# Sums over keys through DRAM into all lanes before the reciprocal, and the mix two slots later

## The chip, the cores and the metric

The kernel runs on one core of one Trainium2 chip. The metric is the device time of one execution in microseconds (us). A core has five engines that the profile names PE (TensorE; PEld are its weight loads), DVE (VectorE), ACT (ScalarE), POOL (GpSimd) and SP (SyncE, which issues every DMA of this kernel). Data lies in SBUF, in PSUM (where PE writes its products) and in DRAM.

## The reference

One layer of a bidirectional encoder, for two sequences: `prompt` with 1024 tokens and `sample` with 2048, of width 1024. The tokens are normalised and projected once; the projection is cut into a pooling mixer, a self-attention with 8 heads of 64 on 2 key heads, a cross-attention of 4 heads into 256 memory tokens, and a gate for each. The gated results are concatenated, projected, normalised and added to the input. What matters here is the softmax of both attentions, and what follows it:

```
s = jnp.einsum('bqkgd,bskd->bkgqs', qblk, k, preferred_element_type=jnp.float32) * scale
p = jax.nn.softmax(s, axis=-1)
return jnp.einsum('bkgqs,bskd->bqkgd', p.astype(v.dtype), v)
...
attn_out = block_self_attention(q, k, v) * jax.nn.silu(g_attn)
...
mix = jnp.concatenate([pool_out, attn_out, x_out], axis=-1)
y = jnp.einsum('bte,ed->btd', mix, w_out)
return x + rms_norm(y, norm_post)
```

## The kernel before

**Stages.** A first stage (about 700 us) normalises and projects all tokens and leaves queries, keys, values and gates in DRAM. The second stage, some 1180 us, does attention, the output projection and the last norm. The change lies in the second.

**Groups and slots.** A `Pair` is 256 tokens; there are 8 pairs of the sample and then 4 of the prompt. Each pair has three `Group`s: kind 0 and kind 1 (self-attention of one key head each) and kind 2 (cross-attention). A group goes over its keys in chunks of 128: 16 chunks for a self-attention group of the sample, 8 for one of the prompt, 2 for kind 2. One chunk of one group is a slot; 344 slots, numbered from 0, follow each other. In the first pair the order is kind 2, 0, 1, in the others 0, 2, 1. A pair of the sample has 34 slots, one of the prompt 18. The groups are numbered from 0 as well; group 9 is kind 0 of the fourth pair (slots 102 to 117), group 10 its kind 2 (118, 119) and group 11 its kind 1 (120 to 135).

**A slot.** For one chunk, `weights` (L212) makes scores S on PE in two halves (L220, or L224 for kind 2) and ACT takes their exponential P (L227) out of PSUM, one half each. The halves have two PSUM buffers. One slot later `sums` (L229) adds P to the running sum z, on DVE alone for the prompt and half on POOL, half on DVE for the sample (L239, L240). In most slots `largest` (L177) also prepares a later group: PE makes scores N (L191, or L183 for kind 2) and DVE reduces them to their largest value (L194). N has two PSUM buffers. Every fourth slot, `values` (L242) multiplies four chunks of P with V on PE (L252); below this is called a value slot.

**The end of a group.** Counted from its first slot n with c chunks: in slot n + c + 1 `totals` (L256) sums z over the partitions on PE (L260) into `zt`, which takes one of the two N buffers. In slot n + c + 2 `take` (L264) multiplies the accumulated values with the gate on DVE (L266), and `inverse` (L269) has DVE take the reciprocal of 128 x 256 elements of `zt` (L272; the 32 lanes of each quarter hold the same sums, so 4 lanes tell all), stores 4 lanes to DRAM (L274) and reads them back, broadcast to 64 lanes each, as `gz` (L278). In slot n + c + 5, or later where the pair before still uses the `mix` tile, `mix_out` (L280) has POOL multiply (L288) and then, one to two slots later, ACT rounds the product (L289) and POOL subtracts for the low part (L290; the instructions themselves carry L416).

**The output projection.** `open_fill` (L423) puts the pieces of a pair's projection on a list, 9 slots after the pair's last slot (L436). Two tiles of 128 tokens each have two halves h of 8 pieces, and a piece is three matmuls (L357 to L359). After each half stands a pause: a slot that takes none. Each slot takes n pieces, so many that the list is done by slot `until`: the pieces left, divided by the slots left less the pauses left, rounded up (L892; `until` is set in L426). For the sample, `until` is the first slot of the next pair + 26, for the prompt + 16 (HOLD, L397). When a half is done in slot s, ACT copies it into the tile y at the end of slot s (`half_out`, L365), squares it in slot s + 1 (L370), and when both halves are there DVE prepares the norm in slot s + 2 (L375) and POOL finishes its root (L63); in slot s + 3 `out` has DVE scale y (L383), POOL add it to `xr`, the input read again (L386), and SP store that. The tiles y and xr have one buffer each (L340, L342): the first half of the next tile cannot be copied before POOL's addition for the tile before is done.

**What sets the order.** The second stage is emitted under a written-out order for PE, ACT, DVE and POOL, which run it as it stands. Within a slot it is: S of half 0 and its exponential; the sums of the chunk before; `largest`; what is due at the slot; S of half 1 and its exponential; the pieces of the projection; what is due at slot + 0.5 (END). SP is not in that list: the order of the DMAs is the planner's, by its own simulated times. The two lines that place the calls on the list, as they stand before:

```
            wait = max(first[g] + g.chunks + 5, free)
            at(wait + END, g.mix_out, wait + END, pair)
        at(max(ends) + 9, open_fill, pair, max(ends) + 9)
...
        at(n + c + 2 + END, g.inverse)
```

Here `free` is the slot from which the mix tile can be used: the pair's first slot + 26 (sample) or + 16 (prompt), and 12 for the first pair.

Of the kernel before, what the change touches and what calls it, by code (L numbers as in the profile page):

```python
# [7 lines left out]
F32 = mybir.dt.float32  # L8
# [15 lines left out]
def encoder(ctx, tc, I, O):  # L24


    nc = tc.nc


    dram = ctx.enter_context(tc.tile_pool(name="scratch", bufs=1, space=DRAM))  # L30
# [102 lines left out]
    class Group:  # L133
# [134 lines left out]

        def inverse(self):  # L269

            r = dbl.tile([128, 256], F32, name="rz", tag="rz", bufs=1)
            nc.vector.reciprocal(out=r, in_=self.zt[:, 0:256])  # L272
            rows = dram.tile([4, 256], F32, name="rows", tag="rows", bufs=4)
            nc.sync.dma_start(out=rows, in_=r[0:128:32])  # L274
            self.gz = dbl.tile([128, 512], F32, name="gz", tag="gz")
            for j in range(2):
                src = rows[2 * j:2 * j + 2].rearrange("l q -> (l q)").unsqueeze(0)
                nc.sync.dma_start(out=self.gz[64 * j:64 * j + 64], in_=src.broadcast_to([64, 512]))  # L278
# [13 lines left out]
    class Pair:  # L292
# [15 lines left out]
        def pool(self, slot):  # L308
            self.mix = [own.tile([128, NC, 2, 128], F32R, name="mix", tag=f"mix{hl}") for hl in range(2)]
            store_mix(slot, self, 0, self.u.rearrange("p c q -> p (c q)"),  # L310
                      self.g.rearrange("p c t q -> p (c t q)"))
# [96 lines left out]
    END = 0.5  # L408

    def at(slot, f, *args):  # L410

        later.setdefault(slot, []).append((f, args))
# [5 lines left out]
    first = {}  # L418
# [9 lines left out]
    for pair in pairs:  # L428
        ends = [first[g] + g.chunks - 1 for g in pair.groups]
        at(min(ends), pair.load_pool)  # L430
        free = 12 if pair is pairs[0] else first[pair.groups[0]] + HOLD[pair.s]
        at(max(min(ends) + 4, free), pair.pool, max(min(ends) + 4, free))
        for g in pair.groups:
            wait = max(first[g] + g.chunks + 5, free)
            at(wait + END, g.mix_out, wait + END, pair)
        at(max(ends) + 9, open_fill, pair, max(ends) + 9)  # L436
    for g in groups:
        n, c = first[g], g.chunks
        at(n + END, g.load_late)
        for k in range(0, c, RUN):  # L440
            ks = list(range(k, min(k + RUN, c)))
            at(n + ks[-1] + 1 + END, g.values, ks)
        at(n + c + 1 + END, g.totals)
        at(n + c + 2, g.take)
        at(n + c + 2 + END, g.inverse)
    for c in range(NC):
        at(4 + 3 * c, load_w_out, c)
        at(7 + 3 * c, split_w_out, c)
# [4 lines left out]
    looks, n = {}, len(slots)  # L453
# [406 lines left out]
    dbl = pool("p2two", 2)  # L860
# [14 lines left out]
    with tc.manual_schedule(engines=order):  # L875
        slot = 0
        while slot < len(slots) or later or fill:
            g, k = slots[slot] if slot < len(slots) else (None, 0)
# [13 lines left out]
            n = -(-(len(fill) - pauses) // max(1, until[0] - slot - pauses)) if fill else 0  # L892
            for _ in range(n):
                x = fill.pop(0)
                if x is None:
                    break
                out, h, c, start, final = x
# [57 lines left out]
```

## Time and profile before

| what | value |
|---|---|
| median of 3 runs | 1884.9 us (1884.27 to 1885.07) |
| the profiled execution | 1885.09 us, of which its span is 1883.0 us |
| mean granted PE clock in it | 0.991 |
| busy, share of the span | PE 96%, DVE 60%, POOL 45%, ACT 37% |

Times in the trace count from the span's start. A row of a timeline gives the start, the duration, the engine, the line, the operation, what it writes and reads, the shape, how many instructions were merged into the row, and, in brackets, how long the engine sat idle before it and who ended that. A row of a table of groups gives the count behind an x, then the summed busy time, the mean duration of one in ns, and the idle time before them. A row of the waits gives who waited for whom, the sum, the number of times and the longest. A row of the windows gives the stretch and its length, then the busy time and the number of instructions for PE, PEld, DVE, ACT and POOL, then the granted PE clock, the share of the DMA engines and GB/s. Matmuls overlap in the trace: rows of 0.39 us start 0.23 us apart.

### The profile page before, as it was taken

How to read it: one execution, taken by the hardware profiler on the slowest of the kernel's cores; microseconds unless marked ns; L12 is line 12 of the kernel's file. 1: busy time of each engine (PE TensorE's matmuls, PEld its weight loads, DVE VectorE, ACT ScalarE, POOL GpSimd, SP SyncE). 2: the span in 40 equal slices, each digit the busy share in tenths (PEclk: the TensorE clock that was granted, in tenths of full speed). 3: DMA queues.
4: the chain of work that ended last, by engine and by line, in shares of the span. 5: the costliest groups of instructions: out<-in, count | busy, mean ns of one | idle time of the engine just before them, and what ended most of it. 6: DMA issues, size and time to landing. Idle time of an engine off the chain costs nothing. (4 is left out here: it accounts for less than half of the span.)

```text
span 1883.0 us, 23531 instructions
## 1 busy us (share of the span) xinstructions
PE 1816.8 (96%) x8520; PEld 1282.0 (68%) x8520; DVE 1131.4 (60%) x1304; ACT 697.3 (37%) x1266; POOL 856.7 (45%) x756
## 2 busy tenths in 40 slices
PE   7999999999999998999999999999999999999996
PEld 6888888988988874465564656556565656565564
DVE  7755146431545167867768676767868576756743
ACT  5523233222422115434434343444434343433331
POOL 3665017520546008845638374664837461413313
PEclk9999999999999999999999999999999999999998
DMA  7634454254433926212122220212222242223211
GB/s 243 201 113 121 109 160 132 76 162 110 116 113 102 216 70 167 68 30 79 46 79 62 70 64 25 79 45 79 62 74 62 67 132 64 91 84 100 86 40 62
DMA packets 148485, 181.83 MB, mean 97 GB/s; under 512 B 21505, under 2 KB 118417, under 8 KB 148369
## 3 DMA queue, kind: packets, MB, share of 16 engines
q1 hardware_dynamic: 148368, 180.33, 33.6%
q8 instruction: 67, 1.10, 0.3%
q14 instruction: 50, 0.40, 0.1%
HBM read 126.50 MB, written 53.62 MB: 96 GB/s over the span
## 5 line engine op out<-in xcount | busy, mean ns | idle before, releaser
L227 ACT ACTIVATE P<-S 128x512 f32<-128x512 f32 x688 | 399.3, 598 | 558.3 <-PE S L220 436.2
L194 DVE TENSOR_REDUCE nb<-N 128x1 f32<-128x1024 f32 x256 | 311.6, 1218 | 240.3 <-PE N L191 239.5
L239 POOL TENSOR_TENSOR z<-z,P 128x512 f32<-128x512 f32 x224 | 316.9, 1415 | 223.7 <-ACT P L227 218.8
L252 PE MATMUL acc<-P,V 128*64 128x512 f32 (+1 forms) x1472 | 320.8, 578 | 0.5
L220 PE MATMUL S<-qa,KA 128*128 128x512 f32 x640 | 275.0, 430 | 9.2 <-ACT P L227 9.2
L240 DVE TENSOR_TENSOR z<-z,P 128x512 f32<-128x512 f32 (+1 forms) x272 | 273.6, 1006 | 12.7 <-ACT P L227 12.3
L63 POOL TENSOR_TENSOR rs<-rs,mhalf 128x1 f32<-128x1 f32 (+2 forms) x100 | 100.4, 1007 | 386.2 <-DVE rs L61 386.1
L220 PE MATMUL S<-qb,KB 65*128 65x512 f32 x640 | 254.5, 398 | 0.0
L548 PE MATMUL pz<-hT_hi,w_hi 128*128 128x512 f32 x592 | 233.2, 394 | 1.4 <-ACT vmst L806 0.8
L549 PE MATMUL pz<-hT_lo,w_hi 128*128 128x512 f32 x592 | 232.3, 392 | 0.0
L550 PE MATMUL pz<-hT_hi,w_lo 128*128 128x512 f32 x592 | 232.1, 392 | 0.2 <-DVE w_lo L69 0.2
L191 PE MATMUL N<-KA,qa 128*128 128x512 f32 x640 | 208.1, 406 | 18.4 <-DVE rz L272 11.7
L252 PEld LDWEIGHTS acc<-P,V 128*64 128x64 f32 x1472 | 98.6, 138 | 180.3 <-issue 171.2
L220 PEld LDWEIGHTS S<-qa,KA 128*128 128x128 f32 x640 | 120.4, 188 | 143.6 <-issue 72.5
L194 DVE TENSOR_REDUCE top<-N 128x1 f32<-128x1024 f32 (+1 forms) x88 | 107.0, 1218 | 96.7 <-PE N L191 76.9
L191 PEld LDWEIGHTS N<-KA,qa 128*128 128x128 f32 x640 | 116.9, 191 | 61.7 <-DVE nb L194 22.1
L548 PE MATMUL pz<-w_hi,hT_hi 128*128 128x384 f32 (+1 forms) x416 | 140.3, 338 | 1.4 <-ACT hT_hi L68 1.4
L549 PE MATMUL pz<-w_lo,hT_hi 128*128 128x384 f32 (+1 forms) x416 | 139.9, 336 | 1.0 <-DVE w_lo L69 0.9
L550 PE MATMUL pz<-w_hi,hT_lo 128*128 128x384 f32 (+1 forms) x416 | 140.1, 338 | 0.0
L357 PE MATMUL py<-wo_hi,mix 128*128 128x512 f32 x352 | 137.7, 391 | 0.0
L358 PE MATMUL py<-wo_lo,mix 128*128 128x512 f32 x352 | 137.6, 391 | 0.0
L359 PE MATMUL py<-wo_hi,mix 128*128 128x512 f32 x352 | 137.4, 390 | 0.0
(116 smaller groups left out, 2487.9 us busy)
## 6 DMA issues: line engine op xcount, KB each, us to landing
wraw<-w_in SPq DMA_DIRECT2D x15, 1536.0 KB
dg<-gst SPq DMA_DIRECT2D x48, 256.0 KB
qa<-dq SPq DMA_DIRECT2D x48, 256.0 KB
gz<-rows SPq DMA_DIRECT2D x72, 128.0 KB
x<-x_sample SPq DMA_DIRECT2D x16, 512.0 KB
xr<-x_sample SPq DMA_DIRECT2D x16, 512.0 KB
y_sample<-xr SPq DMA_DIRECT2D x16, 512.0 KB
dq<-qst SPq DMA_DIRECT2D x96, 64.0 KB
```

Of the source, the lines that this page charges most:

```text
L191: nc.tensor.matmul(S[:, 512 * b:512 * b + 512], lhsT=q, rhs=KA[self.kind][:, k:k + 512], start=True, stop=True)
L194: nc.vector.tensor_reduce(out=out, in_=S, axis=AX.X, op=ALU.max, negate=True)
L220: nc.tensor.matmul(S, lhsT=K[self.kind][rows_, keys], rhs=q, start=n == 0, stop=n == 1)
L227: nc.scalar.activation(out=self.P[k][:, j], in_=S, func=AF.Exp)
L239: nc.gpsimd.tensor_tensor(out=z[:, :cut], in0=a[:, :cut], in1=P[:, :cut], op=ALU.add)
L240: nc.vector.tensor_tensor(out=z[:, cut:], in0=a[:, cut:], in1=P[:, cut:], op=ALU.add)
L252: nc.tensor.matmul(self.acc[64 * j:64 * j + 64, x], lhsT=v, rhs=P[:, j, x], start=(k, i) == (0, 0), stop=k == self.chunks - 1, skip_group_ ...
L357: nc.tensor.matmul(ps, lhsT=mh, rhs=wo_hi[:, c, cols], start=first, stop=False)
L358: nc.tensor.matmul(ps, lhsT=mh, rhs=wo_lo[:, c, cols], start=False, stop=False)
L548: nc.tensor.matmul(ps, lhsT=sh, rhs=mh, start=c == 0, stop=False)
L549: nc.tensor.matmul(ps, lhsT=sh, rhs=ml, start=False, stop=False)
L550: nc.tensor.matmul(ps, lhsT=sl, rhs=mh, start=False, stop=c == n - 1)
```

## The change

`inverse` no longer has DVE take the reciprocal in place. ACT copies `zt` to SBUF, 4 lanes go to DRAM, and come back as a tile `rz` of 128 lanes with 8 columns each. A new call `spread`, two slots later, has DVE take the reciprocal of these 128 x 8 elements, stores them to DRAM and reads them back broadcast, as before. `mix_out` and `open_fill` are put two slots later to make room.

```
         def inverse(self):
 
-            r = dbl.tile([128, 256], F32, name="rz", tag="rz", bufs=1)
-            nc.vector.reciprocal(out=r, in_=self.zt[:, 0:256])
+            t = dbl.tile([128, 256], F32, name="zs", tag="zs", bufs=1)
+            nc.scalar.copy(out=t, in_=self.zt[:, 0:256])
+            sums = dram.tile([4, 256], F32, name="zrows", tag="zrows", bufs=4)
+            nc.sync.dma_start(out=sums, in_=t[0:128:32])
+            self.rz = dbl.tile([128, 8], F32, name="rz", tag="rz")
+            nc.sync.dma_start(out=self.rz, in_=sums.rearrange("l (p x) -> (l p) x", x=8))
+
+        def spread(self):
+            r = self.rz
+            nc.vector.reciprocal(out=r, in_=r)
             rows = dram.tile([4, 256], F32, name="rows", tag="rows", bufs=4)
-            nc.sync.dma_start(out=rows, in_=r[0:128:32])
+            nc.sync.dma_start(out=rows.rearrange("l (p x) -> (l p) x", x=8), in_=r)
             self.gz = dbl.tile([128, 512], F32, name="gz", tag="gz")
...
-            wait = max(first[g] + g.chunks + 5, free)
+            wait = max(first[g] + g.chunks + 7, free)
             at(wait + END, g.mix_out, wait + END, pair)
-        at(max(ends) + 9, open_fill, pair, max(ends) + 9)
+        at(max(ends) + 11, open_fill, pair, max(ends) + 11)
...
         at(n + c + 2 + END, g.inverse)
+        at(n + c + 4 + END, g.spread)
```

## The prediction

> **What bounds the kernel now.** I read the page first, then PE's waits by stage, then the timeline around the waits for the reciprocal, then the granted clock there.
>
> ```profile
> span 1883.0 us, 23531 instructions
> PE 1816.8 (96%) x8520; PEld 1282.0 (68%) x8520; DVE 1131.4 (60%) x1304; ACT 697.3 (37%) x1266; POOL 856.7 (45%) x756
> ```
>
> PE is busy nearly all the time, so a change is worth what it adds to or takes from PE's gaps, and what a gap does to PE's pace. The waits of PE, first for 700 to 1630 us (mostly the sample), then for 1630 us to the end (the prompt):
>
> ```profile
> PE N L191 <- DVE rz L272: 5.8, 10, 0.6
> ...
> PE N L191 <- DVE rz L272: 5.9, 3, 2.0
> ```
>
> These 11.7 us are all that PE waits for the reciprocal: `zt` holds one of the two N buffers until DVE is done. Ten waits are short; three, at the last group of a prompt pair, are long. The next rows show one of those, and a value slot's matmuls undisturbed; then the windows of the half clock after each of the three:
>
> ```profile
> 1706.05 0.39 PE L220 MATMUL S<-qb,KB 65*128 65x512 f32 x1
> 1708.40 1.22 PE L191 MATMUL N<-KA,qa 128*128 128x512 f32 x2 [1.96 <-DVE rz L272]
> 1710.41 5.41 PE L252 MATMUL acc<-P,V 128*64 128x512 f32 x16
> ...
> 1621.79 3.65 PE L252 MATMUL acc<-P,V 128*64 128x512 f32 x16
> ```
> ```profile
> 1635.50:1638.90 3.40, 3.40 (x10) 0.99 (x10) 3.37 (x5) 0.60 (x1) 0.00 (x0) 0.50 0.32 97
> 1707.20:1714.00 6.80, 5.60 (x14) 2.29 (x16) 6.77 (x7) 0.60 (x1) 0.00 (x0) 0.50 0.47 147
> 1782.30:1789.00 6.70, 5.79 (x14) 2.40 (x16) 6.65 (x7) 0.60 (x1) 0.13 (x1) 0.50 0.45 143
> ```
>
> PE works in those windows for 3.40, 5.60 and 5.79 us at clock 0.50, so half of it is lost: 1.7, 2.8 and 2.9 us, together 7.4, on top of the 5.9 us of waiting. A gap of 2 us costs another 2.5 us on average (7.4 / 3).
>
> **The reciprocal leaves DVE's long slot.**
>
> ```profile
> L272 DVE RECIPROCAL rz<-N 128x256 f32<-128x256 f32 x36 | 62.9, 1748 | 4.4 <-PE N L260 3.6 <-DMA rows<-rz 0.8
> L609 ACT COPY z<-pz 128x256 f32<-128x256 f32 x24 | 9.3, 386 | 0.0
> L240 DVE TENSOR_TENSOR z<-z,P 128x1024 f32<-128x1024 f32 x48 | 66.6, 1388 | 9.6 <-ACT P L227 9.3
> L194 DVE TENSOR_REDUCE top<-N 128x1 f32<-128x1024 f32 x64 | 77.7, 1217 | 76.9 <-PE N L191 76.9
> ```
> ```profile
> 1017.41 1.19 ACT L227 ACTIVATE P<-S 128x512 f32<-128x512 f32 x2 [0.28 <-PE S L220]
> 1018.69 1.75 DVE L272 RECIPROCAL rz<-N 128x256 f32<-128x256 f32 x1
> 1020.49 0.73 PE L191 MATMUL N<-KA,qa 128*128 128x512 f32 x2 [0.61 <-DVE rz L272]
> ```
>
> DVE gives back 1.75 us in each of 36 groups. Its 8 columns are 8/256 of 1748 ns, 0.05 us; with an estimate for the start I take 0.15. ACT gains a copy, 0.39 us by L609. It stands behind the first of the two exponentials of 1017.41 and ends near 1018.4, two microseconds before the reciprocal's end at 1020.44, and PE's N at 1020.49 goes on without the 0.61 us. The second exponential ends 0.39 us later, at 1019.0; were PE to wait for it, that is 0.4 us in a group at most. So the ten short waits go: **minus 5.8 us**. The three long ones and their half clock are worth 13.3 us (5.9 + 7.4), but DVE there has 2.6 us of work in each slot (the sum of L240, 1.39 us, and the reduction of L194, 1.22) against 1.4 us on PE (six matmuls 0.23 us apart), and catches up now also because PE stands still. I hand back 0.6 us for each, **minus 11.5 us**, with bounds of 8 and 13.3.
>
> **The new trip, and DVE's wait at `spread`.** The trip as it is, from store to use:
>
> ```profile
> 1020.46 0.56 SPq L274 DMA_DIRECT2D rows<-rz  x1
> 1022.12 1.10 SPq L278 DMA_DIRECT2D gz<-rows  x2
> 1025.66 1.28 POOL L288 TENSOR_TENSOR o<-o,gz 128x512 f32<-128x512 f32 x1 [3.54 <-DMA gz<-rows]
> ```
>
> The store takes 1.66 us until the next DMA may start, the broadcast 3.0 us from its second issue (1022.63). The new first half takes 1.66 us and then, for 4 KB in pieces of 32 bytes, which no row shows, between these two: 3.4 to 4.7 us from 1018.4, to some 1023. DVE comes to `spread` behind the reduction of slot n + c + 4, near 1022.4, so it waits up to 0.7 us (more if SP first issues a gate load). Behind DVE stand a sum and a reduction, but this is the value slot, in which PE is busy for 3.65 us; I count nothing, and up to 0.7 us for each prompt pair in the bound above. The second half ends 6 us later, before POOL's multiply two slots later, so POOL's wait of 3.54 us goes, worth nothing on PE.
>
> Once the cover is gone: group 0, while the weights load.
>
> ```profile
> 715.30 1.22 DVE L194 TENSOR_REDUCE nb<-N 128x1 f32<-128x1024 f32 x1
> 716.62 0.54 SPq L274 DMA_DIRECT2D rows<-rz  x1
> 724.53 1.10 SPq L278 DMA_DIRECT2D gz<-rows  x2
> 721.86 0.63 PE L191 MATMUL N<-KA,qa 128*128 128x512 f32 x2
> 708.00:722.00 14.00, 12.81 (x57) 6.80 (x50) 11.41 (x12) 6.87 (x12) 6.56 (x5) 1.00 1.03 267
> ```
>
> The DMA engines are full until 722, and a 4 KB store took 7.9 us (716.62 to 724.53). DVE's `spread` stands behind the reduction of 715.30. If the sums are back at 725, a sum and a reduction later (2 us) PE gets its N buffer at 727 instead of 721.86: 5 us, and 2 for the clock. If the copy's earlier store slips ahead of the loads, nothing. **Plus 5 us**, between 0 and 8.
>
> **The mix and the projection two slots later.** This moves POOL's multiply, ACT's rounding and POOL's low part, but the mix of a pair's first two groups is mostly held by `free` anyway. It also moves where the projection's pieces lie. Take the third pair: its list opened in slot 110 and must be done by 128. Before, slots 111 on took 3, 3, 2, 3, 3, 2 pieces; after a pause the next half began in 118. The first tile was done in 116, its `out` came in 119, and the second tile's first half was done in 121. Now it opens in 112: 32 pieces in 128 - 113 - 4 = 11 slots gives 3, and from 113 on 3, 3, 2, 3, 3, 2, 3, 3, 2. The first tile is done in 118, its `out` comes in slot **121**, and the second tile's first half is done in slot **121** as well. ACT's copy of that half must wait until POOL has added the first tile (one y buffer). Slots 119, 121 and 122 as they were:
>
> ```profile
> 1066.06 0.51 PE L224 MATMUL S<-qa,KA 128*128 128x256 f32 x2
> 1067.31 1.22 DVE L194 TENSOR_REDUCE nb<-N 128x1 f32<-128x1024 f32 x1 [4.52 <-PE N L191]
> 1068.45 1.27 DVE L383 SCALAR_TENSOR_TENSOR y<-y,rs,npost 128x1024 f32<-128x1024 f32 x1
> 1069.81 2.79 POOL L386 TENSOR_TENSOR xr<-xr,y 128x1024 f32<-128x1024 f32 x1 [6.39 <-DVE y L383]
> 1074.62 0.50 PE L220 MATMUL S<-qa,KA 128*128 128x512 f32 x1
> 1077.78 0.59 ACT L365 COPY y<-py 128x512 f32<-128x512 f32 x1 [0.86 <-PE py L359]
> 1078.16 0.50 PE L220 MATMUL S<-qa,KA 128*128 128x512 f32 x1
> 1079.66 0.43 PE L220 MATMUL S<-qa,KA 128*128 128x512 f32 x1
> 1080.68 0.73 PE L191 MATMUL N<-KA,qa 128*128 128x512 f32 x2 [0.36 <-DVE nb L194]
> 1083.10 0.40 PE L220 MATMUL S<-qa,KA 128*128 128x512 f32 x1
> ```
>
> POOL's addition ended 6.54 us after the start of `out`'s slot (1066.06 to 1072.60). Put `out` into slot 121: ACT's copy starts 6.54 us after that slot's start instead of 3.16 (1077.78 - 1074.62), and ends at 7.13. Behind it on ACT stands the first exponential of slot 122, 0.60 us, at 7.73, and for its buffer waits PE's first S of slot 123, which is due 5.04 us after the start of slot 121 (1079.66 - 1074.62). Slot 122 is the pause, so PE has nothing else: a gap of 2.7 us. Slot 123 (1079.66 to 1083.10, 3.44 us) has 0.65 us more than its 12 matmuls need (2.79), a wait behind DVE's reciprocal and reduction that disappears in the gap; net 2.05 us. To this comes the clock, 2.5 us by the three windows, as this gap is longer than theirs: 4.5 us. The same count of slots holds for the second to seventh pair. In the first, `out` comes in 52 and the copy at the end of 53, a slot of cover. **Plus 27 us** (6 x 4.5), 18 to 33 for gaps of 2.1 to 3.3 us and 1.7 to 2.9 for the clock.
>
> The Trainium skill weighs against the clock's part: "TensorE: Matmul & The Clock Gate", section "Why this matters for your kernels", advises no PE-idle gaps over about 3 us, one idle window bringing the clock back to half. By that, a gap of 2.7 us keeps the full clock. This trace disagrees: three gaps of 2.0 us out of three were followed by clock 0.50.
>
> For the four pairs with 8 pieces to a slot (the last of the sample, three of the prompt) the same copy already waits:
>
> ```profile
> 1603.54 0.58 ACT L365 COPY y<-py 128x512 f32<-128x512 f32 x1 [5.62 <-POOL xr L386]
> 1604.68 0.50 PE L220 MATMUL S<-qa,KA 128*128 128x512 f32 x1 [0.54 <-ACT P L227]
> ```
>
> Eight pieces, 5.5 us of matmuls (24 x 0.23), hide it but for half a microsecond. There the pieces now fill four slots in a row; the copy comes one slot later, behind as many pieces: zero, within 4 us in all. In the last pair all pieces come at the end:
>
> ```profile
> 1860.47 1.29 POOL L416 TENSOR_TENSOR mix<-o,mix 128x512 fp32r<-128x512 f32 x1 [0.73 <-ACT mix L416]
> ...
> 1872.18 0.39 PE L359 MATMUL N<-wo_hi,mix 128*128 128x512 f32 x1
> ```
>
> The 24 matmuls that need the last mix are the last, 5.4 us up to 1872.4, so from 1867 on; it is there at 1861.8. DVE's `take` sets the start of both trips, and the new one has 5 us to spare: zero.
>
> **Sum.** -5.8 - 11.5 + 5 + 27 = +14.7. The profiled execution, 1885.1 us, is 0.2 over the median of 1884.9, so the prediction is 1899.6.
>
> **Rivals.**
> *The copy is not held.* If POOL's addition ended 3.4 us sooner, the six gaps vanish: 1885 - 17.3 + 5 = 1873, faster. For it: in 40 of its 44 copies ACT waits for PE's pieces, in four for POOL. Against: those four are just the ones whose `out` comes in the copy's own slot. It decides once the addition ends less than 4 us after the slot's start. 0.13.
> *The gaps come without the half clock.* Then 6 x 2.05 = 12.3 stands against 12.3 of net gain: 1885, no change. This is what the cited page's rule makes of it; three windows speak against. 0.08.
> *DVE's wait at `spread` becomes the bound.* If the trip takes 8 us, the 11 groups at a pair's end past group 0's pair hold DVE 4 us in the value slot, of which 2 are hidden: 2 us and the clock each, +50: 1949. The 1.66 us of the store speaks against. 0.06.
> *The early copy doesn't free the buffer sooner* (held by something later): no gain, 1885 + 5 + 27 = 1917. 0.05.
> My forecast has 0.68.
>
> **Chances and range.** A difference under 0.2% (3.8 us) can't be told from none here. Slower 0.68 + 0.06 + 0.05 = 0.79, same 0.08, faster 0.13. My sum's own bounds: 1885 + 18 + 0 - 19 = 1884 to 1885 + 33 + 8 - 14 = 1912; with 1917 of the last rival, 1883 to 1917 leaves out 0.13 + 0.06.
>
> **What would show it.** Right: ACT's y copies waiting for POOL's xr ten times, six of them near 4 us; PE gaps of 2 to 3 us behind ACT's exponential once in each of pairs 2 to 7, each with a window at clock 0.50; no wait of PE for DVE's reciprocal; the windows at 1635, 1707 and 1782 gone; a wait of DVE for `rz` near 716 of some 8 us. Wrong: pairs 2 to 7 (109 us long) not longer, or DVE's waits for `rz` above 2 us in every group.

## The result

The changed kernel takes 1905.3 us (median of 4 runs, 1901.4 to 1908.3) against 1885.0 for the kernel before on the same chip: 1.010 times as long, with a 95% interval from 1.0083 to 1.0118. The prediction, 1899.6, had the sign and a time 5.7 us too low. The profiled execution, the slowest of the four, took 1908.3 us. Its page gives:

```profile
PE 1824.1 (96%) x8520; PEld 1291.0 (68%) x8520; DVE 1080.2 (57%) x1304; ACT 707.0 (37%) x1302; POOL 858.9 (45%) x756
```

DVE has 51 us less work and the kernel is slower: DVE's total was never the limit. PE's 8520 matmuls are the same; the difference lies in PE's gaps and in its clock.

PE's waits after the change, for 700 to 1630 us and for 1630 us to the end; then the two waits of DVE and ACT on which the prediction staked most:

```profile
PE S L220 <- ACT P L227: 17.2, 24, 2.5
PE N L191 <- DVE nb L194: 9.3, 10, 6.3
...
PE acc L252 <- DVE o L266: 2.3, 1, 2.3
...
PE acc L252 <- DVE o L266: 6.4, 3, 2.3
PE S L220 <- ACT P L227: 5.8, 10, 1.2
...
DVE rz L280 <- DMA rz<-zrows: 26.0, 10, 10.1
...
ACT y L373 <- POOL xr L394: 44.1, 9, 5.7
```

The wait for DVE's reciprocal, 11.7 us before, is gone from the list. In its place stand a wait of 6.3 us at the start, waits of 2.5 us behind ACT's exponential (forecast), and waits behind DVE's `take` (L266), which I had not forecast.

The table gives, for each profiled execution, the length of three stretches of the second stage: from the first score matmul of slot 0 to that of slot 34, from there to that of slot 272, and from there to the end of the last score matmul, in slot 343. What lies before and after them stands beside. Up to slot 0 the edits change no computation; that part differs by up to 3.7 us from run to run. The profiled execution need not be near the median: for after, e7 and e11 it is the slowest run. The experiments are in the same table and are told below.

| kernel | to slot 0 | slots 0 to 33 | sample, 34 to 271 | prompt, 272 to 343 | tail | median of the runs |
|---|---|---|---|---|---|---|
| before | 698.5 | 91.7 | 759.4 | 290.4 | 43.0 | 1885.0 |
| after | 700.9 | 98.1 | 765.7 | 299.8 | 42.1 | 1905.3 |
| e1 list back | 700.6 | 96.0 | 752.9 | 282.3 | 42.0 | 1875.4 |
| e2 shift only | 698.5 | 90.9 | 776.4 | 303.4 | 42.1 | 1913.2 |
| e4 group 0 old | 698.4 | 91.1 | 770.9 | 294.2 | 42.0 | 1898.4 |
| e5 take early | 700.0 | 97.6 | 766.0 | 286.6 | 42.2 | 1895.2 |
| e6 out early | 699.0 | 97.5 | 754.4 | 297.8 | 42.5 | 1892.6 |
| e7 kind-2 mix | 699.3 | 94.1 | 772.3 | 294.6 | 41.8 | 1899.2 |
| e9 list back, group 0 old | 700.5 | 91.3 | 753.0 | 282.2 | 41.7 | 1870.4 |
| e10 copy only | 700.9 | 90.8 | 755.1 | 284.5 | 42.9 | 1876.1 |
| e11 four repairs | 697.2 | 93.1 | 757.5 | 292.6 | 41.9 | 1880.7 |
| e12 mix back too | 699.6 | 92.5 | 754.4 | 306.4 | 41.9 | 1895.3 |

From before to after the start loses 6.4 us, the sample 6.3, the prompt 9.4. The sample's loss comes after a gain: the value slots at the end of a group, 5.95 us long before, take 5.10.

**The start.** The timeline of after, the trip of group 0:

```profile
718.64 0.54 SPq L274 DMA_DIRECT2D zrows<-zs  x1
725.27 0.33 SPq L276 DMA_DIRECT2D rz<-zrows  x1
727.33 0.20 DVE L280 RECIPROCAL rz<-rz 128x8 f32<-128x8 f32 x1 [10.05 <-DMA rz<-zrows]
728.57 1.21 DVE L194 TENSOR_REDUCE nb<-N 128x1 f32<-128x1024 f32 x1
729.84 0.80 PE L191 MATMUL N<-KA,qa 128*128 128x512 f32 x1 [6.32 <-DVE nb L194]
```

A store of 4 KB takes 6.6 us until its load is issued, while the weights fill the DMA engines (their share is 1.0 in these 6.6 us), and the load takes 2.1 us; DVE stands 10 us, and behind it the reduction for which PE waits. That is the chain as forecast: DVE starts 2.3 us later than the 725 forecast, but slot 0 itself starts 2.4 us later in this trace than in that of before.

**The sample.** The timeline of after where the first half of the second tile is copied, from the third pair's list; then the four other PE rows of the same kind:

```profile
1083.74 1.23 DVE L194 TENSOR_REDUCE nb<-N 128x1 f32<-128x1024 f32 x1 [3.44 <-PE N L191]
1084.88 1.28 DVE L391 SCALAR_TENSOR_TENSOR y<-y,rs,npost 128x1024 f32<-128x1024 f32 x1
1086.24 2.75 POOL L394 TENSOR_TENSOR xr<-xr,y 128x1024 f32<-128x1024 f32 x1 [5.31 <-DVE y L391]
1089.02 0.59 ACT L373 COPY y<-py 128x512 f32<-128x512 f32 x1 [4.22 <-POOL xr L394]
1090.16 0.50 PE L220 MATMUL S<-qa,KA 128*128 128x512 f32 x1 [2.45 <-ACT P L227]
...
980.01 0.50 PE L220 MATMUL S<-qa,KA 128*128 128x512 f32 x1 [2.45 <-ACT P L227]
1201.90 0.50 PE L220 MATMUL S<-qa,KA 128*128 128x512 f32 x1 [2.45 <-ACT P L227]
1312.10 0.50 PE L220 MATMUL S<-qa,KA 128*128 128x512 f32 x1 [2.45 <-ACT P L227]
1423.83 0.50 PE L220 MATMUL S<-qa,KA 128*128 128x512 f32 x1 [2.45 <-ACT P L227]
```

The chain is the forecast one: DVE scales y, POOL adds, ACT copies, the exponential follows, PE waits; 2.45 us where 2.7 was worked out. But there are five such gaps and not six. In the place of the sixth:

```profile
1520.11 1.28 DVE L391 SCALAR_TENSOR_TENSOR y<-y,rs,npost 128x1024 f32<-128x1024 f32 x1 [0.67 <-POOL rs L63]
1521.47 2.37 POOL L394 TENSOR_TENSOR xr<-xr,y 128x1024 f32<-128x1024 f32 x1 [1.40 <-DVE y L391]
1526.80 0.59 ACT L373 COPY y<-py 128x512 f32<-128x512 f32 x1 [0.79 <-PE py L367]
```

No `largest` is due in those slots, so DVE has no reduction ahead of the scaling and starts as soon as POOL's root is there; POOL is done at 1523.84 and ACT waits for PE's pieces, not for POOL.

**The prompt.** Before, the first values of each kind-2 group lay behind eight pieces of the projection, in which DVE did the `take` that frees the accumulator (one PSUM buffer). Two slots later the pieces are elsewhere. The timeline of after at one of four such places, and the windows there (PE's work in its first bracket, the clock third from the end):

```profile
1668.82 0.39 PE L220 MATMUL S<-qb,KB 65*128 65x512 f32 x1
1671.48 0.69 PE L252 MATMUL acc<-P,V 128*64 128x256 f32 x2 [2.27 <-DVE o L266]
```
```profile
1668.03:1671.44 3.41, 1.18 (x6) 0.62 (x4) 3.40 (x3) 1.46 (x3) 0.58 (x1) 1.00 0.89 227
1671.44:1674.85 3.41, 3.37 (x16) 1.71 (x16) 0.00 (x0) 0.00 (x0) 0.00 (x0) 0.50 0.28 83
```

PE stands 2.27 us and then works 3.4 us at half clock.

### The profile page after: what moved, and what is told of

It is laid out like the page before. It is cut to its first block, busy times and chain, and to the rows that moved or that the text cites. A ratio compares the mean times of both kernels' runs of the same rounds, so it can differ in the third digit from the quotient of the medians.

```text
span 1906.5 us, 23736 instructions
## 1 busy us (share of the span) xinstructions
PE 1824.1 (96%) x8520; PEld 1291.0 (68%) x8520; DVE 1080.2 (57%) x1304; ACT 707.0 (37%) x1302; POOL 858.9 (45%) x756
## 4 chain that ended last, share of the span: by engine, by line
PE 70%; issue 11%; DVE 7%; POOL 5%; DMA 4%; ACT 2%; SPq 1%; POOLq 0%; ACTq 0%; DVEq 0%
PE acc L252 13%; PE S L220 10%; PE pz L559 10%; PE pz L557 9%; PE pz L558 9%; PE N L191 5%; PE py L365 3%; PE py L366 3%; PE py L367 3%; DVE z L240 2%; POOL z L239 1%; DVE nb L194 1%; POOL xr L394 1%; DVE y L391 1%; PE S L224 1%
## 5 line engine op out<-in xcount | busy, mean ns | idle before, releaser
L239 POOL TENSOR_TENSOR z<-z,P 128x512 f32<-128x512 f32 x224 | 327.0, 1460 | 190.0 <-ACT P L227 183.8
L240 DVE TENSOR_TENSOR z<-z,P 128x512 f32<-128x512 f32 (+1 forms) x272 | 267.8, 985 | 32.1 <-ACT P L227 31.6
```

What stands on the lines that cost most here:

```text
L239: nc.gpsimd.tensor_tensor(out=z[:, :cut], in0=a[:, :cut], in1=P[:, :cut], op=ALU.add)
L240: nc.vector.tensor_tensor(out=z[:, cut:], in0=a[:, cut:], in1=P[:, cut:], op=ALU.add)
```

## The experiments

The theory, once the traces had been compared: the trip through DRAM does what it is for; what costs is the shift of the mix and of the list by two slots, in the sample through the y copy and in the prompt through two more collisions, plus the first group's wait. The rival: the trip itself costs, by its DMAs, its copy on ACT and DVE's new wait. All medians of the experiments are of 4 to 12 runs beside runs of the kernel before on the same chip, whose median was 1884.7 to 1885.6.

**One part at a time.** e1 takes after and puts the list back, and the mix to half a slot behind its old place:

```
-            wait = max(first[g] + g.chunks + 7, free)
+            wait = max(first[g] + g.chunks + 5.5, free)
-        at(max(ends) + 11, open_fill, pair, max(ends) + 11)
+        at(max(ends) + 9, open_fill, pair, max(ends) + 9)
```

> The kernel after, with the projection's list opened 9 slots behind the pair again and the mix of a group at its end + 5.5 slots (half a slot later than before the change) instead of 7. The trip of the sums through DRAM stays. Theory (the shift costs, the trip gains): against before's 1885.0 us, minus 7.7 for the end-group value slots of the sample (9 x 0.86 in the trace of after), minus 10.7 for the three prompt value slots (3.42, 4.41, 2.83), plus 7.4 for group 0, so about 1874, between 1868 and 1880; the five gaps of 2.45 us and the waits of PE for DVE's take at the prompt's kind-2 values are gone. Rival (the trip itself costs: its DMAs and ACT's copy delay the rest, the shift is innocent): 1895 or more, with the gaps of after still there.

Measured: 1875.4 us, 0.9942 of before (0.9928 to 0.9955): with the shift undone the trip makes the kernel faster, as the theory had it. e2 takes before and makes only the shift, the same two lines as in the change, with the reciprocal in place:

> The kernel before, its reciprocal in place on DVE, with only the mix and the list of the projection two slots later. Theory (the shift costs): plus 13.5 us for the gaps behind the y copy in pairs 2 to 6 and plus 10 to 18 for the prompt, where the values of kind 2 lose the projection's pieces as their cover and the value slots keep their wait for the reciprocal, so 1908 to 1918. Rival (the trip is the cause): 1885 within 4. A third case, that DVE's longer queue moves everything and the y copy no longer meets POOL's addition: 1890 to 1900, without gaps of 2 us in pairs 2 to 6.

Measured: 1913.2 us, 1.0156 of before (1.0134 to 1.0178). PE's waits in e2, for 700 to 1630 us and from 1630 us on, and ACT's:

```profile
PE S L220 <- ACT P L227: 17.2, 24, 2.5
PE N L191 <- DVE rz L272: 5.6, 10, 0.6
...
PE acc L252 <- DVE o L266: 6.4, 3, 2.3
...
ACT y L365 <- POOL xr L386: 44.1, 9, 5.7
```

The waits behind ACT and behind the `take` and the nine copies held by POOL are those of after, to the tenth, without any trip. So the shift makes them, and the rival falls for all but the first group. With it, e1 and the table size the terms: from e1 to after, the sample loses 12.8 us (765.7 less 752.9) and the prompt 17.5 (299.8 less 282.3). Without the trip, from before to e2, the sample loses 17.0 and the prompt 13.0: the sum is the same within 0.3 us, the parts are not. (In e2's prompt PE no longer waits for the reciprocal itself, but 7.0 us, in three places, for a reduction that DVE does ahead of it.)

The value slot that was the prompt's long wait, in e1 (slot 312; before it took 9.93 us, with N waiting 1.96 us and the matmuls at half clock):

```profile
1703.77 0.39 PE L220 MATMUL S<-qa,KA 128*128 128x512 f32 x1
...
1708.86 0.50 PE L220 MATMUL S<-qa,KA 128*128 128x512 f32 x1
```

It takes 5.09 us. That is the gain of the change, 4.84 us in one slot.

**The single collisions.** Each of the next four mends one of them in after.

e4: the first group keeps its reciprocal in place and makes no trip.

```
+            if self.n == 0:
+                nc.vector.reciprocal(out=t, in_=self.zt[:, 0:256])
...
+                nc.sync.dma_start(out=rows, in_=t[0:128:32])
```

> The kernel after, but the first group of the second stage takes its reciprocal in place on DVE and makes no trip of its sums; the other 35 groups as in after. Theory (DVE waits 10.1 us for the sums behind the weight loads, PE 6.3 us for DVE, and half a clock follows): minus 7.4 us from 1905.3, so about 1898 (1895 to 1901), and no wait of PE over 2 us near 730. Rival (the weight loads hold PE there in any case): 1905 within 2.

Measured: 1898.4 us (1895.7 to 1899.5), the stretch of slots 0 to 33 at 91.1 instead of 98.1. PE's wait for DVE's reductions from 700 to 1630 us (in after 9.3 us, the longest 6.3), and DVE's remaining waits for the other 35 trips:

```profile
PE N L191 <- DVE nb L194: 3.9, 10, 1.0
...
DVE rz L288 <- DMA rz<-zrows: 10.8, 8, 4.4
```

The wait was the trip's, not the loads'. e5 has the `take` half a slot earlier:

```
-        at(n + c + 2, g.take)
+        at(n + c + 1 + END, g.take)
```

> The kernel after, with every group's take (the gate's multiply, which frees the accumulator) half a slot earlier on DVE, right behind the totals. Theory (the four prompt waits of PE for that multiply, 8.6 us together, are real gaps, and the half clock at 1671, 1746 and 1825 follows from them, 1.7 + 3.4 + 1.7 us): minus 8 to minus 15 from 1905.3, so about 1894. Rival (what waits is the accumulation itself, or the next wait behind it takes its place, the exponentials or the N buffer): 1901 to 1906, with gaps of the same length under another name.

Measured: 1895.2 us (1894.1 to 1897.7). The prompt's stretch falls from 299.8 to 286.6, and PE waits for `take` nowhere any more. The four gaps were 2.3 + 6.4 = 8.7 us of waiting in after's list; the rest, 4.5, is clock, less what other slots give back: from slot 272 to 1830 us the clock is 0.50 for six steps of 3.41 us in after (the last section tells of these steps) and for one in e5. e6 has `out` half a slot earlier:

```
-                        at(slot + 3, out.out)
+                        at(slot + 2 + END, out.out)
```

> The kernel after, with the projection's out (DVE's scaling of y, POOL's addition to xr, the store) half a slot earlier, at the end of the slot in which the norm is prepared. Theory (ACT's y copy of the second tile waits for that addition, and PE for ACT): the five gaps of 2.45 us shrink to about 0.8 and the half clock behind two of them goes, 5 x 1.7 + 2 x 1.0, about minus 10 from 1905.3, so 1895 (1892 to 1899). Rival 1 (the copy waits for the pieces or for ACT's own queue): 1903 to 1907, the gaps as long as before. Rival 2 (DVE now stands before POOL's root and holds the sums behind it): 1905 to 1912, with new waits of DVE for POOL.

Measured: 1892.6 us (1891.6 to 1896.9). PE's wait behind ACT for 700 to 1630 us, and ACT's wait for POOL:

```profile
PE S L220 <- ACT P L227: 4.4, 20, 0.3
...
ACT y L373 <- POOL xr L394: 23.0, 4, 5.8
```

The five gaps are gone altogether, the five held copies with them (nine to four), and the sample's stretch falls by 11.3 us. It was the y tile. e7 puts the mix of kind 2 one slot back:

```
-            wait = max(first[g] + g.chunks + 7, free)
+            wait = max(first[g] + g.chunks + (6 if g.kind == 2 else 7), free)
```

> The kernel after, with only the mix of the kind-2 groups one slot earlier (their end + 6 slots instead of 7), which in the prompt puts it back into the slot that it had before the change. Theory (in the prompt POOL's multiply for kind 2 stands behind the addition to xr, ACT's rounding behind that, and the exponentials behind the rounding: three PE gaps of 1.25 us in slots 292, 310 and 328): minus 4 from 1905.3 (3 x 1.41), down to minus 8 if the half clock at 1801 goes too, so 1897 to 1902. Rival (PE catches up in the value slot that follows, where it then waits for ACT or DVE in any case): 1904 to 1907.

Measured: 1899.2 us (1896.5 to 1904.0). The waits behind ACT from 1630 us on fall:

```profile
PE S L220 <- ACT P L227: 2.0, 7, 0.4
```

They were 5.8 us, up to 1.2. In its profiled execution the prompt gained 5.2 us while the sample, whose instructions stand as in after, lost 6.6: the same five gaps, with other windows of half clock behind them (last section). The runs of e7 and of after overlap (after: 1901.4 to 1908.3), so it is the wait that shows the collision, more than the time.

**What the gain is.** e10 adds to before one thing, ACT's copy; DVE's long instruction stays where it was:

```
-            nc.vector.reciprocal(out=r, in_=self.zt[:, 0:256])
+            nc.scalar.copy(out=r, in_=self.zt[:, 0:256])
+            nc.vector.reciprocal(out=r, in_=r)
```

> The kernel before, with one thing added: ACT copies the totals out of the N buffer and DVE takes the reciprocal of all 128 x 256 elements from that copy in SBUF, in the same place of its queue. No trip of the sums, no shift of the mix or the list. It parts the two halves of the gain: the N buffer that comes free sooner, and the 1.75 us that leave DVE. If the held buffer alone made the waits: as the run with the list back without its first group's cost, 1867 to 1870. If DVE's long instruction made them (its reductions still come 1.75 us later, and PE waits for those instead): 1880 to 1886, with waits of 2 us for DVE's reductions at the three prompt value slots and the half clock behind them. Between: the sample's nine value slots gain 0.86 each (1877) and the prompt's do not.

Measured: 1876.1 us (1872.9 to 1876.2), 0.9945 of before (0.9933 to 0.9957). Slot 312 in e10, then PE's waits there from 1630 us on for DVE's reductions and for the rows of a query:

```profile
1700.71 0.40 PE L220 MATMUL S<-qa,KA 128*128 128x512 f32 x1
...
1705.81 0.50 PE L220 MATMUL S<-qa,KA 128*128 128x512 f32 x1
```
```profile
PE N L191 <- DVE top L194: 3.3, 4, 1.3
...
PE S L224 <- DMA qb<-rows: 0.7, 1, 0.7
```

The slot takes 5.10 us, as with the trip. So these slots waited for the held N buffer; that PE would wait 2 us for the reductions instead, my second case, does not come. The time is near the 1877 of the third case, but not for its reason: the prompt's long slots gain in full, and part comes back later, above all 3.9 us in slot 334. There PE waits 0.7 us for the rows of a query: SP issues their loads at 1779.67 us, behind the store and the broadcast of the reciprocal, while in e9 it issues them at 1774.90, ahead of both. A half clock of 6.83 us follows. Sample and prompt together are 10.2 us shorter than before; with the trip (e9, next) 14.6. By that comparison, in which the mix also stands half a slot apart, the trip is worth some 4 us more than the copy alone. But 3.0 of them lie in slot 334, by SP's order and the half clock; so what the 1.6 us that leave DVE in each group are worth by themselves stays open.

**Together.** e9 is e1 with the first group of e4:

> Two edits together: the list of the projection and the mix placed as in the run with the list back, and the first group's reciprocal in place on DVE. Theory (the two costs lie in different stretches and add up): 1875.4 less 7.4, about 1868 (1865 to 1871), faster than both kernels. Rival (once the start is shorter, something later holds the rest back): 1873 or more.

Measured: 1870.4 us (1868.7 to 1871.3), 0.9921 of before (0.9908 to 0.9933): faster than both kernels, and the best version found. e11 goes the other way: the shift stays, and the four repairs e4 to e7 are put together.

> The kernel after with its shift of two slots kept, and the four repairs that were tried singly put together: the first group's reciprocal in place, take half a slot earlier, out half a slot earlier, the kind-2 mix one slot earlier. Theory (four separate collisions make up the loss, and little else): 1905.3 less 6.9, 10.1, 12.8 and 6.1 is 1869.4; as the half clock behind some gaps was counted in more than one of them, 1868 to 1875. Rival (the repairs cover for each other, and the shift has a cost of its own that none of them touches): 1880 or more.

Measured: 1880.7 us (1878.6 to 1884.2), 0.9978 of before. The single repairs sum to 35.9 us, together they give 24.6; so the rival is right: against e9 10.3 us are left. In the profiled executions (that of e11 is the slowest of 12) the prompt is 10.4 us longer than in e9 and the sample 4.5. In the prompt PE now waits for a reduction of DVE before the totals, and once for a sum (the list from 1630 us on), and the half clock lasts three windows in its first pair:

```profile
PE N L260 <- DVE top L194: 4.3, 2, 2.1
PE N L260 <- DVE z L240: 4.1, 1, 4.1
```
```profile
1622.49:1625.90 3.41, 1.81 (x6) 0.84 (x6) 3.41 (x3) 1.25 (x3) 3.41 (x2) 1.00 0.09 37
1625.90:1636.14 10.24, 9.05 (x30) 6.22 (x30) 9.76 (x10) 3.24 (x6) 3.49 (x3) 0.50 0.42 142
```

In the trace the sum that DVE does ahead of that reduction, at 1623.54 us, takes 2.27 us, while POOL works beside it; the 28 such sums of e11 with POOL idle take 1.2 each. That would be half of the wait of 2.1 us. It is a reading of the trace; no run tried it.

**Does the trip need room?** e12 is e9 with the mix where it stood before the change, half a slot earlier (`5` for `5.5`).

> The run with the list back and group 0 in place, with the mix half a slot earlier still, where it stood before the change (the group's end + 5 slots); the trip stays. In the run before it PE has gaps of 1.47 us behind ACT in slots 285, 303 and 321, where ACT rounds the mix between two exponentials, and the kernel before has none there. If the trip is back in time: minus 2.8 (3 x 0.93) and up to minus 2.4 for the slots after the prompt's groups, so 1865 to 1868 against 1870.4. If gz lands later than POOL wants it (the trip needs the room that the change made for it): POOL waits 1 to 3 us for gz, ACT's rounding with it, and the time is 1870 to 1876.

Measured: 1895.3 us (1893.9 to 1900.3). The rival's direction, and far beyond its price: the prompt's stretch is 306.4 us, 24 more than in e9. The timeline of e12 at one of four places:

```profile
1721.67 0.50 SPq L297 DMA_DIRECT2D gz<-rows  x1
1725.28 1.26 POOL L307 TENSOR_TENSOR o<-o,gz 128x512 f32<-128x512 f32 x1 [10.93 <-DMA gz<-rows]
1726.58 0.62 ACT L435 CAST mix<-o 128x512 fp32r<-128x512 f32 x1 [4.38 <-POOL o L307]
1727.74 0.58 PE L224 MATMUL S<-qa,KA 128*128 128x256 f32 x1 [3.07 <-ACT P L227]
```

The broadcast is issued at 1721.67; POOL's multiply waits for it until 1725.28, ACT's rounding for POOL, the exponentials stand behind the rounding on ACT, and PE runs dry. With the trip the mix has to come later, but half a slot is enough (e9), and the list needs no move at all.

## Why the prediction was right, and where its terms were not

- *Ten short waits and three long ones, 17.3 us of gain.* Right in kind: no PE wait for DVE's reciprocal is left. The half clock in the long slots is gone in e1 and e9; in after the third of them (slot 330) still takes 7.26 us, as a half clock that begins at 1801 us, before it, reaches into it. In e9, where nothing covers it, sample and prompt together gain 14.6 us against before (6.4 and 8.2). Each long slot is shorter by 3.8 to 5.0 us in e1, and 0.8 to 1.0 come back in a later slot of the pair, where I had taken 0.6. Another 0.9 come back in the slot in which ACT rounds the mix; e10, with the mix in its old place, has none of that, so it belongs to the half slot and not to the trip.
- *Group 0, plus 5, up to 8.* Right: 6.9 us by e4, 5.0 from e1 to e9. The chain was the forecast one, and the 5 and 2 us that I had named for it add up to 7.
- *The y copy, plus 27.* The chain was right in every link, with nine held copies instead of ten and gaps of 2.45 us instead of 2.7. The term was mis-sized: 12.8 us by e1, 11.3 by e6, and 17.0 from before to e2, where a half clock follows all five gaps. One of six gaps is missing, as no reduction stood ahead of DVE's scaling there, and the 2.5 us of clock were too much: two of five gaps have half clock behind them in after, and 17.0 us for five gaps is 3.4 each where 4.5 was forecast.
- *"zero, within 4 us in all" for the pairs with 8 pieces to a slot.* This step failed. I followed the copy and not what the pieces had covered. In the prompt the shift costs 17.5 us from e1 to after: up to 13.2 of it go with an earlier `take` (e5), 5.2 with an earlier kind-2 mix (e7). The moves of the list and of the mix were both in the change as I described it; I never asked which wait the eight pieces hid in the slots that they left.
- *The spread's wait, hidden.* Right in that past group 0 no wait of PE follows from it, but the waits are longer than the 0.7 us that I allowed: past group 0 the nine other waits of DVE sum to 15.9 us, 1.8 on average and up to 4.8. e9, which has such waits as well (7.6 us), is the fastest kernel.
- *The rivals.* That the copy isn't held falls with the nine held copies of after. That DVE's wait would be the bound falls with e9, that the early copy frees nothing with e10. That the gaps keep the full clock was half right: behind two of the five came half clock.

So that the total came out near was luck: a term too large by 14 us stood beside one too small by 17.5. For the shift 27 + 0 was forecast, and 12.8 + 17.5 was measured.

## What to carry to other kernels

When a block of work is moved in a written-out order, price the place that it leaves as well as the place to which it goes: list each wait that it covered there. Before a result is sent on a longer way to relieve an engine, ask whether the engine's time or the buffer that it holds is what others wait for; here a copy of 0.4 us by itself brought 9.5 of the 15.2 us of the best version, with no trip to wait for. A move made "for room" is to be tried in small steps: here half a slot of the two was enough, and each half slot more can meet other work.

## What the runs showed of the hardware

I had priced a gap of 2 us at 2.5 us of clock, from three cases in which a half clock seemed to follow the gap. In two of the three it begins before the gap ends: the gap at 1708.40 lasts from 1706.44, and the half clock begins at 1707.16. The half clock follows a grid instead. In every trace of this case the windows with clock 0.50 past 700 us begin at whole multiples of 3.413 us from each other and last one, two or three such steps (but for the last one of a trace). The same gap of 2.45 us, in after, once inside one step and once cut by a boundary; the second row of each couple is the step that follows:

```profile
1087.77:1091.18 3.41, 1.02 (x4) 0.87 (x5) 2.01 (x4) 2.16 (x5) 3.33 (x3) 1.00 0.39 154
1091.18:1094.60 3.42, 3.42 (x9) 2.65 (x8) 2.75 (x3) 1.38 (x4) 1.67 (x2) 0.50 0.75 208
1200.41:1203.83 3.42, 1.93 (x8) 1.62 (x9) 2.01 (x4) 3.07 (x8) 2.84 (x3) 1.00 0.59 204
1203.83:1207.24 3.41, 3.41 (x16) 2.75 (x15) 3.08 (x4) 1.57 (x3) 2.33 (x2) 1.00 0.65 211
```

With 2.4 us of a step idle the next runs at half clock; with 1.5 it doesn't. I cut the time from 700 to 1830 us of all 12 traces (the two kernels and ten experiments) into the steps of each trace's own grid. Of the steps at full clock with PE idle for 1.75 us or more, 52 of 52 were followed by half clock; with 1.25 to 1.75 us idle, 14 of 34; with 0.5 to 1.25 us, 1 of 212. The one exception is the half clock of e10's slot 334, after a step with 0.9 us idle. So what counts is not the length of a gap but the idle time, of one gap or several, that falls into one step, with a border near half of the step. In e2 a pair lasts about 33 steps (33 x 3.413 = 112.64 us, and the windows at 1198.89 and 1311.53 are 112.64 apart), so each gap falls on nearly the same place of its step, and all five are followed by half clock:

```profile
1195.48:1198.89 3.41, 1.60 (x7) 1.34 (x8) 3.41 (x4) 2.67 (x6) 3.15 (x3) 1.00 0.52 183
1198.89:1202.30 3.41, 3.41 (x10) 2.63 (x9) 2.11 (x3) 0.60 (x1) 1.44 (x1) 0.50 0.67 210
1308.12:1311.53 3.41, 1.42 (x6) 1.20 (x7) 3.41 (x4) 2.55 (x6) 3.33 (x3) 1.00 0.52 169
1311.53:1314.94 3.41, 3.41 (x10) 2.63 (x9) 2.29 (x3) 0.71 (x2) 1.45 (x2) 0.50 0.72 219
```

The sample's stretch of the same code took 765.7 us in after, 770.9 in e4 and 772.3 in e7; it holds 2, 6 and 7 steps of half clock in these traces. The Trainium skill, "TensorE: Matmul & The Clock Gate", in its Part 1, describes a free-running window of 3413 ns; the grid here agrees, with steps of 3.41 us. Its section "Why this matters for your kernels" advises against PE-idle gaps over about 3 us, as one window of idle brings the clock back to half. That limit is too wide here: steps with 1.75 us idle were enough. This comes from counting traces; no experiment moved a gap across a boundary on purpose.
